# MLP up product of a GLA/gMLP block: pairs of column blocks as seven products of quarters, sums on GpSimd

## The chip, the cores and the metric

The kernel runs on one NeuronCore of a Trainium2 chip. The metric is device time of one launch in microseconds (us), the median of several runs. Engines are called as the profile calls them: PE is TensorE, DVE VectorE, ACT ScalarE, POOL GpSimd, SP SyncE, which issues most DMAs.

## The reference, cut to what matters

One layer of an encoder in float32, 256 rows (SEQ) of width 2048 (D_MODEL). The change lies in the MLP at its end:

```python
h = h + mixed @ w_out[l]
hn = rmsnorm(h, norm_mlp_w[l])
h = h + jnp.square(jax.nn.relu(hn @ w_ff_up[l])) @ w_ff_down[l]   # 2048 x 8192, 8192 x 2048
return rmsnorm(h, norm_final_w)
```

Ahead of it stand the projections of the normed input (`w_in`), a gated linear attention, a spatial gating unit, their gated merge (`w_branch`) and `w_out`.

## The kernel before

Every large product keeps float32 accuracy with three products of rounded operands: an operand is split into a high part (rounded to the `F32R` type) and a low part (the rest), and PE computes high x high, low x high and high x low into one PSUM bank. `gemm` (L188) makes one block of 512 output columns (CB) for 256 rows: 16 tiles of the inner dimension (KT), taken in pairs, and two halves of the rows (NTT), so 16 x 2 x 3 = 96 matmuls of 512 columns. The activations are the stationary operand, the weights stream.

For each pair of tiles `split_weights` (L173) loads 128 x 1024 weights by SP into a tile `w` (5 buffers), ACT casts them into `wh` (4 buffers, L182) and DVE subtracts to make `wl` (4 buffers, L183). `wh` and `wl` come free when PE has used them, so the three engines run a few pairs ahead of PE and no more.

The MLP has four stages of 2048 hidden columns. `up` (L737) makes a block of hidden columns: a `gemm` with the normed rows `hT` (the norm's weight is in `hT`, the row's factor `rstd2` is applied by ACT on the way out of PSUM with Relu), a square on DVE (L740), and jobs that turn the block into a stationary operand: 16 transposes of 32 x 256 on DVE (L271) and a split (L288 on ACT, L289 on DVE). Jobs wait in `pending`, and `gemm` runs one of them (`drain`) per pair of tiles. `down` (L750) multiplies the hidden columns of the stage before with a block of `w_ff_down` and adds the result into `h` on DVE (L755). Blocks of `up` and `down` alternate. After the first block of the kernel, a scheduler orders the instructions of each engine, and engines run their queues in order.

POOL has only small work: the powers of -0.5 in the norms (`rsqrt_of`, L309), on tiles of one or two columns, and memsets. In the spatial gating unit (L675 to L698) DVE has statistics (L685), scalings (L689), products with a weight (L694) and a split (L697) between the low parts L183.

Of the kernel before, what the change touches and what calls it, by code (L numbers as in the profile page):

```python
# [14 lines left out]
P = 128  # L15
# [24 lines left out]
W_ROW = 1088  # L40
# [18 lines left out]
def block_kernel(  # L59
# [25 lines left out]
    slots = ctx.enter_context(tc.tile_pool(name="slots", bufs=29))  # L85
# [87 lines left out]
    def split_weights(src, by_k=False):  # L173
# [6 lines left out]
        for s in [slice(i, i + 1) for i in range(k)] if by_k else [slice(0, k)]:  # L180
            nc.sync.dma_start(wv[:, s], src[:, s])  # L181
            pin(nc.scalar.copy(hv[:, s], wv[:, s]))  # L182
            pin(nc.vector.tensor_tensor(  # L183
                lv[:, s], wv[:, s], hv[:, s].bitcast(F32), op=ALU.subtract
            ))
        return hv, lv

    def gemm(a, w, c0, n=CB, parts=1, k0=0, after=None, split_tail=False):  # L188
# [5 lines left out]
        def products(kt, tt, hi, lo):  # L194
            ah, al = a.at(kt, tt)
            for i in range(parts):
                o = ps[i][tt][:, 0:m]
                wh = hi[:, kt % 2, cols(i, m)]
                wl = lo[:, kt % 2, cols(i, m)]
                pin(nc.tensor.matmul(o, lhsT=ah, rhs=wh, start=kt == 0, stop=False))  # L200
                pin(nc.tensor.matmul(o, lhsT=al, rhs=wh, start=False, stop=False))  # L201
                pin(nc.tensor.matmul(o, lhsT=ah, rhs=wl, start=False, stop=kt == KT - 1))  # L202

        for kb in range(KT // 2):
            r0 = k0 + kb * 2 * P
            hi, lo = split_weights(
                w[r0 : r0 + 2 * P, c0 : c0 + n].rearrange("(k p) n -> p k n", p=P),
                by_k=after is not None and kb == 0,
            )
# [6 lines left out]
            if split_tail and kb >= KT // 2 - 3:  # L216
# [12 lines left out]
    def to_operand_pair(dst, src, scale=None):  # L229
# [11 lines left out]
        hi, lo = dst.hi[-1], dst.lo[-1]  # L241
        if scale is None:
# [30 lines left out]
    def to_operand_vector(dst, src, scale=None):  # L273

        tr = []

        def step(jm):
            if jm == 0:
                tr.append(slot())
            transpose_quadrants(tr[0], src, jm)  # L280

        def split():
# [92 lines left out]
    vec_m = cpool.tile([NVEC, P], F32, name="vec_m")  # L375
# [418 lines left out]
    for st in range(n_st + 1):  # L794
# [48 lines left out]
```

## Time and profile before

| what | value |
|---|---|
| median of 3 runs | 1625.09 us (1625.01 to 1626.37) |
| profiled execution, its own time | 1625.84 us |
| its span, first to last instruction | 1624.1 us |
| PE busy | 1606.1 us, 99% |
| DVE busy | 1128.0 us, 69% |
| ACT busy | 755.9 us, 47% |
| POOL busy | 23.3 us, 1% |
| mean granted TensorE clock | 0.998 |

The span is what the profile's instructions cover; the time of the execution has 1.7 us around it. Busy time of PE is modelled, so the pace of PE is better read from how far apart other engines' regular work starts.

### The profile page before, as it was taken

Reading aid. Unit: us, or ns where it says so; the run is one execution under the profiler, and the core shown is the slowest. Engines: PE = TensorE matmul, PEld = TensorE weight load, DVE = VectorE, ACT = ScalarE, POOL = GpSimd, SP = SyncE. Lnnn points to the kernel's source line nnn. Section 1 sums busy time; section 2 is a strip of 40 time slices with the busy share of each in tenths; the row PEclk is TensorE's granted clock in tenths of the full one; section 3 lists DMA queues with packets and bytes.
Section 4 is the critical chain, followed back from the end, with each engine's and each line's share of the span. In section 5 each row is a group of like instructions: output and inputs, shape, how many; then the busy total and the mean of one; then the engine's idle time right before and its main releaser. Section 6 shows DMA issues by size and latency. Waiting matters only on the chain.

```text
span 1624.1 us, 19352 instructions
## 1 busy us (share of the span) xinstructions
PE 1606.1 (99%) x7224; PEld 1330.5 (82%) x7224; DVE 1128.0 (69%) x1486; ACT 755.9 (47%) x864; POOL 23.3 (1%) x50
## 2 busy tenths in 40 slices
PE   8999999999999999999999999999999999999997
PEld 6877888888888888888888888888888888888886
DVE  5759576855555788877759788876666666677754
ACT  6475444544444444544435544444444444444443
POOL 0000000000000000000000000000000000000000
PEclk9999999999999999999999999999999999999999
DMA  7655566566666666566655656655555666666653
GB/s 246 205 167 172 154 193 182 182 216 199 200 209 184 193 190 185 182 211 200 200 193 180 199 179 195 207 194 192 184 184 194 195 205 199 197 193 193 219 193 116
DMA packets 163095, 311.75 MB, mean 192 GB/s; under 512 B 9812, under 2 KB 13192, under 8 KB 163000
## 3 DMA queue, kind: packets, MB, share of 16 engines
q1 hardware_dynamic: 160016, 306.35, 60.2%
q10 hardware_dynamic: 2984, 4.16, 0.7%
q8 instruction: 56, 0.92, 0.2%
q14 instruction: 39, 0.32, 0.1%
HBM read 308.37 MB, written 2.10 MB: 191 GB/s over the span
## 4 chain that ended last, share of the span: by engine, by line
PE 97%; DVE 1%; DMA 0%; issue 0%; ACT 0%; SPq 0%; POOL 0%; ACTq 0%; POOLq 0%; DVEq 0%
PE mm L200 32%; PE mm L202 32%; PE mm L201 32%; DVE slot L271 1%; PE tr L564 1%; DVE wl L183 1%; PE tr L612 1%; DMA h<-in_x_dram 0%; PE tr L707 0%; PE tr L239 0%; ACT wh L182 0%; PE tr L467 0%; POOL col L309 0%; SPq L181 0%; PE tr L415 0%
## 5 line engine op out<-in xcount | busy, mean ns | idle before, releaser
L183 DVE TENSOR_TENSOR wl<-w,wh 128x1024 fp32r<-128x1024 f32 (+2 forms) x577 | 700.6, 1222 | 432.0 <-ACT wh L182 427.2
L182 ACT CAST wh<-w 128x1024 fp32r<-128x1024 f32 (+2 forms) x577 | 605.4, 1051 | 732.5 <-PE mm L201 683.4
L200 PE MATMUL mm<-wh,slot 128*128 128x512 f32 (+1 forms) x2336 | 905.3, 388 | 0.0
L202 PE MATMUL mm<-wl,slot 128*128 128x512 f32 (+1 forms) x2336 | 902.9, 387 | 2.3 <-DVE wl L183 2.3
L201 PE MATMUL mm<-wh,slot 128*128 128x512 f32 (+1 forms) x2336 | 902.6, 386 | 0.0
L202 PEld LDWEIGHTS mm<-wl,slot 128*128 128x128 f32 x2336 | 438.5, 188 | 93.6 <-DVE wl L183 4.5
L200 PEld LDWEIGHTS mm<-wh,slot 128*128 128x128 f32 x2336 | 438.9, 188 | 88.3 <-ACT pair L329 0.2
L201 PEld LDWEIGHTS mm<-wh,slot 128*128 128x128 f32 x2336 | 438.9, 188 | 87.8
L271 DVE STREAM_TRANSPOSE slot<-pair 32x256 f32<-32x256 f32 x496 | 216.2, 436 | 8.3
L329 ACT ACTIVATE pair<-mm,rstd 128x512 f32<-128x512 f32 x58 | 39.9, 689 | 31.6 <-PE mm L202 31.4
L288 ACT CAST slot<-slot 128x1024 fp32r<-128x1024 f32 x23 | 24.3, 1056 | 32.3 <-DVE slot L271 32.3
L309 POOL TENSOR_TENSOR col<-col,mhalf 128x1 f32<-128x1 f32 (+1 forms) x20 | 17.9, 897 | 859.8 <-DVE col L307 572.4
L289 DVE TENSOR_TENSOR slot<-slot,slot 128x1024 fp32r<-128x1024 f32 x23 | 28.0, 1219 | 0.0
L755 DVE TENSOR_TENSOR h<-mm,h 128x512 f32<-128x512 f32 x32 | 22.0, 692 | 5.3 <-PE mm L202 5.3
L271 DVE STREAM_TRANSPOSE slot<-h 32x256 f32<-32x256 f32 x48 | 21.0, 436 | 0.9
L293 ACT ACTIVATE slot<-slot,vec 128x256 fp32r<-128x256 f32 x28 | 12.1, 498 | 16.4 <-DVE slot L271 16.4
L740 DVE TENSOR_TENSOR pair<-pair 128x1024 f32<-128x1024 f32 x16 | 19.5, 1219 | 0.0
L315 ACT ACTIVATE ev<-h 128x512 f32<-128x512 f32 x24 | 15.0, 627 | 7.9 <-DVE h L755 7.9
L254 DVE SCALAR_TENSOR_TENSOR slot<-tr,mixw,slot 128x256 fp32r<-128x256 f32 x16 | 7.0, 479 | 11.2 <-ACT slot L249 11.2
L294 DVE SCALAR_TENSOR_TENSOR slot<-slot,vec,slot 128x256 fp32r<-128x256 f32 x28 | 11.8, 479 | 0.0
L249 ACT ACTIVATE slot<-tr,mixw 128x256 fp32r<-128x256 f32 x16 | 6.7, 471 | 10.6 <-PE tr L239 10.6
L710 DVE SCALAR_TENSOR_TENSOR pair<-tr,vec,pair 128x256 f32<-128x256 f32 x16 | 7.0, 479 | 6.5 <-PE tr L707 6.4
(103 smaller groups left out, 265.2 us busy)
## 6 DMA issues: line engine op xcount, KB each, us to landing
w<-in_w_in_dram SPq DMA_DIRECT2D x215, 512.0 KB, 3.7
w<-in_w_ff_up_dram SPq DMA_DIRECT2D x128, 512.0 KB, 3.7
w<-in_w_ff_down_dram SPq DMA_DIRECT2D x128, 512.0 KB, 3.5
w<-in_w_branch_dram SPq DMA_DIRECT2D x64, 512.0 KB, 3.5
w<-in_w_out_dram SPq DMA_DIRECT2D x32, 512.0 KB, 3.6
w<-in_w_in_dram SPq DMA_DIRECT2D x8, 528.0 KB, 4.6
h<-in_x_dram SPq DMA_DIRECT2D x8, 256.0 KB, 7.8
bg<-in_b_gate_dram ACTq DMA_DIRECT2D x8, 256.0 KB, 4.0
```

Source lines behind the costliest of these rows:

```text
L182: pin(nc.scalar.copy(hv[:, s], wv[:, s]))
L183: pin(nc.vector.tensor_tensor(lv[:, s], wv[:, s], hv[:, s].bitcast(F32), op=ALU.subtract))
L200: pin(nc.tensor.matmul(o, lhsT=ah, rhs=wh, start=kt == 0, stop=False))
L201: pin(nc.tensor.matmul(o, lhsT=al, rhs=wh, start=False, stop=False))
L202: pin(nc.tensor.matmul(o, lhsT=ah, rhs=wl, start=False, stop=kt == KT - 1))
L271: nc.vector.transpose(dv[cols(jm, 32), i], sv[cols(i, 32), jm])
L288: nc.scalar.copy(hi, tr[0])
L289: nc.vector.tensor_tensor(lo, tr[0], hi.bitcast(F32), op=ALU.subtract)
L309: nc.gpsimd.tensor_tensor(r, m, mhalf[:, 0:width], op=ALU.pow)
L329: nc.scalar.activation(res[:, tt, :], ps[tt], func, scale=scale[tt])
L740: nc.vector.tensor_tensor(a, a, a, op=ALU.mult)
L755: nc.vector.tensor_tensor(part, ps[tt], part, op=ALU.add)
```

## The change

The hidden columns come in eight stages of 1024 instead of four of 2048. `hidden(0)` makes the first two blocks of `up` as before. The other seven stages are made by `strassen`: the normed rows are a 2 x 2 matrix of quarters (128 rows x 1024 inner), the weights another (1024 inner x 512 columns), and their product is formed from seven products of quarters instead of eight, by Winograd's form of Strassen's scheme. Each product has 8 inner tiles and three matmuls per tile, as before, into one bank of PSUM; seven of the eight banks are in use.

The seven sums of the left side are prepared once, in jobs during the first two blocks: `norm_step` applies norm weight and row factor to kept raw rows (`raw`), `split_left` splits quarters and sums, `left_sum` makes four sums on POOL. The sums of weights are made anew in each of the four steps of a stage: POOL adds b00+b01 into `s1`, then b01+b11, b00+b01, b10+b00 in place, 128 x 1024 each; ACT casts and DVE subtracts for each of the seven products. At the end of a stage seven adds on DVE (L882) put the products together, and Relu and square are on ACT.

`down` takes 8 inner tiles at a time, so a block has 48 matmuls and there are twice as many blocks. Of its four low parts per block the last three are made on POOL (except in the last stage). In the first two blocks of `up` every second low part is on POOL. A block of 528 columns elsewhere is loaded in two halves, since the weight tile is now 1024 wide.

```diff
 C_G = 10256
 
 
-W_ROW = 1088
+W_ROW = 1024
...
+    def subtract(dst, a, b, gpsimd=False):
+        return (nc.gpsimd if gpsimd else nc.vector).tensor_tensor(dst, a, b, op=ALU.subtract)
+    def split_weights(src, by_k=False, gpsimd=False):
...
-                lv[:, s], wv[:, s], hv[:, s].bitcast(F32), op=ALU.subtract
-            ))
+            pin(subtract(lv[:, s], wv[:, s], hv[:, s].bitcast(F32), gpsimd))
         return hv, lv
...
-    def gemm(a, w, c0, n=CB, parts=1, k0=0, after=None, split_tail=False):
+    def gemm(a, w, c0, n=CB, parts=1, k0=0, nk=KT, after=None, split_tail=False, on_gpsimd=(), jobs=1):
 
...
+            src = w[r0 : r0 + 2 * P, c0 : c0 + n].rearrange("(k p) n -> p k n", p=P)
+            hi, lo = [], []
+            step = 2 if n <= CB else 1
+            for k in range(0, 2, step):
+                hv, lv = split_weights(
+                    src[:, k : k + step], by_k=after is not None and kb == 0,
+                    gpsimd=kb in on_gpsimd,
+                )
+                hi += [hv[:, i, :] for i in range(step)]
+                lo += [lv[:, i, :] for i in range(step)]
...
             if kb > 1 or kb == 1 and len(pending) > 6:
-                drain()
+                drain(jobs)
...
         hi, lo = dst.hi[-1], dst.lo[-1]
+        if keep is not None:
+            if k == 0:
+                keep.append(slot())
+            nc.scalar.copy(keep[-1][:, k : k + 2, :], tv)
...
-    def up(st, j, f):
-        ps = gemm(hT, w_ff_up[0], st * D + j * CB)[0]
-        a = scaled(ps, rstd2, AF.Relu)
-        nc.vector.tensor_tensor(a, a, a, op=ALU.mult)
-        to_operand_vector(f, a)
...
+    row_scale = ev_tile()[:, 0:T]
+    def row_scale_step():
+        tp = tr_ps()
+        for tt in range(NTT):
+            wide = ev_tile()[:, 0:P]
+            nc.scalar.activation(wide, ident, AF.Identity, scale=0.0, bias=rstd2[tt])
+            nc.tensor.matmul(tp[:, cols(tt, P)], lhsT=wide, rhs=ident, start=True, stop=True)
+        nc.vector.tensor_copy(row_scale, tp[:, 0:T])
+    def norm_step(b):
+        for k in range(4):
+            v = raw[b][:, k, :]
+            nc.vector.scalar_tensor_tensor(
+                out=v, in0=v, scalar=vcol(V_MLP + 4 * b + k), in1=row_scale,
+                op0=ALU.mult, op1=ALU.mult,
+            )
...
+    left = {}
+    def split_left(name, src):
+        hi, lo = slot(F32R), slot(F32R)
+        for s, hv, lv in zip(src, halves(hi), halves(lo)):
+            nc.scalar.copy(hv, s)
+            nc.vector.tensor_tensor(lv, s, hv.bitcast(F32), op=ALU.subtract)
+        left[name] = [t.rearrange("p a (s t) -> p (a s) t", t=P) for t in (hi, lo)]
+    sums = []
+    def left_sum(name, a, b, op):
+        if not sums:
+            sums.append(slot())
+        for d, x, y in zip(halves(sums[0]), a(), b()):
+            nc.gpsimd.tensor_tensor(d, x, y, op=op)
+        split_left(name, halves(sums[0]))
+    def last_sum():
+        return halves(sums[0])
+    prepare = [row_scale_step] + [lambda b=b: norm_step(b) for b in range(4)]
+    for i, j in ((0, 0), (0, 1), (1, 1)):
+        prepare.append(lambda i=i, j=j: split_left(f"A{i}{j}", quarter(i, j)))
+    for name, a, b, op in (
+        ("A10-A11", lambda: quarter(1, 0), lambda: quarter(1, 1), ALU.subtract),
+        ("A10-A11-A00", last_sum, lambda: quarter(0, 0), ALU.subtract),
+        ("A10-A11-A00+A01", last_sum, lambda: quarter(0, 1), ALU.add),
+        ("A00-A10", lambda: quarter(0, 0), lambda: quarter(1, 0), ALU.subtract),
+    ):
+        prepare.append(lambda name=name, a=a, b=b, op=op: left_sum(name, a, b, op))
...
+    def strassen(w, c0):
+        bank = {n: mm_ps() for n in "1235"}
+        bank.update({n: tr_ps() for n in "764"})
+        def product(i, name, a, src):
+            hi, lo = pair_of("wh", F32R, 4), pair_of("wl", F32R, 4)
+            nc.scalar.copy(hi, src)
+            subtract(lo, src, hi.bitcast(F32))
+            ah, al = left[a]
+            for kk in range(2):
+                kt = 2 * i + kk
+                for n, (x, y) in enumerate(((ah, hi), (al, hi), (ah, lo))):
+                    nc.tensor.matmul(
+                        bank[name], lhsT=x[:, kt, :], rhs=y[:, kk, :],
+                        start=kt == 0 and n == 0, stop=kt == SK - 1 and n == 2,
+                    )
+        def add(dst, x, y):
+            nc.gpsimd.tensor_tensor(dst, x, y, op=ALU.add)
+        for i in range(SK // 2):
+            b = []
+            for kh, nh in ((0, 0), (1, 0), (1, 1), (0, 1)):
+                t = ring_tile("b", 4) if kh == 0 else pair_of("w", F32, 5)
+                r0, n0 = kh * SK * P + i * 2 * P, c0 + nh * CB
+                load(t, w[r0 : r0 + 2 * P, n0 : n0 + CB].rearrange("(k p) n -> p k n", p=P))
+                b.append(t)
+            b00, b10, b11, b01 = b
+            s1 = ring_tile("s", 1)
+            add(s1, b00, b01)
+            add(b01, b01, b11)
+            product(i, "1", "A00", b00)
+            product(i, "2", "A01", b10)
+            product(i, "3", "A10-A11-A00+A01", b11)
+            product(i, "5", "A10-A11", s1)
+            add(b00, b00, b01)
+            product(i, "7", "A00-A10", b01)
+            product(i, "6", "A10-A11-A00", b00)
+            add(b10, b10, b00)
+            product(i, "4", "A11", b10)
+            drain(3)
+        p1, u2, u3, t = (ev_tile() for _ in range(4))
+        c = [pair_tile() for _ in range(2)]
+        nc.scalar.copy(p1, bank["1"])
+        for dst, x, y, op in (
+            (c[0][:, 0, :], bank["2"], p1, ALU.add),
+            (u2, bank["6"], p1, ALU.add),
+            (u3, bank["7"], u2, ALU.add),
+            (t, bank["3"], u2, ALU.subtract),
+            (c[0][:, 1, :], bank["4"], u3, ALU.add),
+            (c[1][:, 1, :], bank["5"], u3, ALU.subtract),
+            (c[1][:, 0, :], bank["5"], t, ALU.add),
+        ):
+            nc.vector.tensor_tensor(dst, x, y, op=op)
+        return c
+    def hidden(st):
+        f = Operand()
+        c0 = st * 2 * CB
+        if st == 0:
+            pending.extend(prepare)
+            for j in range(2):
+                ps = gemm(hT, w_ff_up[0], c0 + j * CB, on_gpsimd=(1, 3, 5, 7), jobs=2)[0]
+                a = scaled(ps, rstd2, AF.Relu)
+                nc.vector.tensor_tensor(a, a, a, op=ALU.mult)
+                to_operand_vector(f, a)
+        else:
+            for a in strassen(w_ff_up[0], c0):
+                nc.scalar.activation(a, a, AF.Relu)
+                nc.scalar.activation(a, a, AF.Square)
+                to_operand_vector(f, a)
+        return f
...
     def down(st, j, f):
         last = st == n_st - 1
-        ps = gemm(f, w_ff_down[0], j * CB, k0=st * D, split_tail=last and j == 3)[0]
+        ps = gemm(
+            f, w_ff_down[0], j * CB, k0=st * SK * P, nk=SK, split_tail=last and j == 3,
+            on_gpsimd=() if last else (1, 2, 3),
+        )[0]
...
+    prev = hidden(0)
+    for st in range(1, n_st + 1):
+        f = hidden(st) if st < n_st else None
...
         for j in range(4):
-            if st < n_st:
-                up(st, j, f)
-            if prev is not None:
-                down(st - 1, j, prev)
+            down(st - 1, j, prev)
```

POOL in the MLP. In the kernel before, its rows from the norm after `w_out` to the end are these (`col` is one value per row, `mhalf` the constant -0.5):

```order
L309 TENSOR_TENSOR col_7320<-col_7318,mhalf 128x1
L309 TENSOR_TENSOR col_7328<-col_7326,mhalf 128x1
L779 TENSOR_TENSOR col_12490<-col_12488,mhalf 128x1
L779 TENSOR_TENSOR col_12509<-col_12507,mhalf 128x1
```

In the changed kernel POOL's rows at the end of the first `down` stage and the start of the second Strassen stage are these (L178 is a low part, L847 a sum of weights; `slot_7808` and `slot_7904` hold b00, `slot_7814` and `slot_7910` b01, `slot_7816` is `s1`, the `w` tiles b10 and b11):

```order
L178 TENSOR_TENSOR wl_8456<-w_8454,wh_8455 128x1024
L178 TENSOR_TENSOR wl_8474<-w_8472,wh_8473 128x1024
L847 TENSOR_TENSOR slot_7816<-slot_7808,slot_7814 128x1024
L847 TENSOR_TENSOR slot_7814<-slot_7814,w_8528 128x1024
L178 TENSOR_TENSOR wl_8496<-w_8494,wh_8495 128x1024
L847 TENSOR_TENSOR slot_7808<-slot_7808,slot_7814 128x1024
L847 TENSOR_TENSOR w_8526<-w_8526,slot_7808 128x1024
L847 TENSOR_TENSOR slot_7816<-slot_7904,slot_7910 128x1024
```

The first two sums of a stage stand ahead of the last low part of `down`; from there on POOL has only sums, four a step, 16 a stage.

DVE in the MLP. In the kernel before, its rows in a block of `up` (with the jobs of the block before it) are of this kind:

```order
L183 TENSOR_TENSOR wl_8569<-w_8567,wh_8568 128x1024
L740 TENSOR_TENSOR pair_8502<-pair_8502 128x1024
L271 STREAM_TRANSPOSE slot_8550<-pair_8502 32x8x32 x8
L183 TENSOR_TENSOR wl_8591<-w_8589,wh_8590 128x1024
L271 STREAM_TRANSPOSE slot_8550<-pair_8502 32x8x32 x4
L183 TENSOR_TENSOR wl_8613<-w_8611,wh_8612 128x1024
L271 STREAM_TRANSPOSE slot_8550<-pair_8502 32x8x32 x4
```

In the changed kernel they are these at the start of the second Strassen stage (the low parts of products 1, 2, 3, 5, 7, 6, 4 in that order, then those of the next step):

```order
L178 TENSOR_TENSOR wl_8534<-slot_7808,wh_8533 128x1024
L178 TENSOR_TENSOR wl_8544<-w_8526,wh_8543 128x1024
L178 TENSOR_TENSOR wl_8554<-w_8528,wh_8553 128x1024
L918 TENSOR_TENSOR h<-mm_8434,h 128x512
L918 TENSOR_TENSOR h<-mm_8435,h 128x512
L178 TENSOR_TENSOR wl_8564<-slot_7816,wh_8563 128x1024
L178 TENSOR_TENSOR wl_8575<-slot_7814,wh_8574 128x1024
L178 TENSOR_TENSOR wl_8585<-slot_7808,wh_8584 128x1024
L178 TENSOR_TENSOR wl_8596<-w_8526,wh_8595 128x1024
L178 TENSOR_TENSOR wl_8614<-slot_7904,wh_8613 128x1024
```

Three low parts stand ahead of the last adds of `down` into `h`; after them DVE has nothing but low parts until the end of the stage, and those of products 6 (`slot_7808`) and 4 (`w_8526`) read what POOL writes. The transposes now lie between the rows of `down`.

## Rows read from the trace of the kernel before

**Rows 1.** The page: busy time by engine, and the chain that ended last.

```profile
PE 1606.1 (99%) x7224; PEld 1330.5 (82%) x7224; DVE 1128.0 (69%) x1486; ACT 755.9 (47%) x864; POOL 23.3 (1%) x50
PE 97%; DVE 1%; DMA 0%; issue 0%; ACT 0%; SPq 0%; POOL 0%; ACTq 0%; POOLq 0%; DVEq 0%
```

**Rows 2.** Timeline of DVE in the MLP: start, duration, instruction, [idle before, releaser].

```profile
1042.15 1.22 DVE L183 TENSOR_TENSOR wl<-w,wh 128x1024 fp32r<-128x1024 f32 x1
1043.29 1.22 DVE L289 TENSOR_TENSOR slot<-slot,slot 128x1024 fp32r<-128x1024 f32 x1
1044.42 2.35 DVE L183 TENSOR_TENSOR wl<-w,wh 128x1024 fp32r<-128x1024 f32 x2
...
1053.21 1.22 DVE L183 TENSOR_TENSOR wl<-w,wh 128x1024 fp32r<-128x1024 f32 x1 [1.49 <-ACT wh L182]
1055.93 1.23 DVE L183 TENSOR_TENSOR wl<-w,wh 128x1024 fp32r<-128x1024 f32 x1 [1.50 <-ACT wh L182]
1058.65 1.23 DVE L183 TENSOR_TENSOR wl<-w,wh 128x1024 fp32r<-128x1024 f32 x1 [1.49 <-ACT wh L182]
```

**Rows 3.** Windows: busy us of each engine in a stretch, granted clock, DMA.

```profile
1130.00:1216.00 86.00, 86.00 (x381) 71.22 (x380) 58.80 (x72) 36.93 (x38) 0.00 (x0) 1.00 0.61 195
```

**Rows 4.** Groups by line and shape: count, busy us, mean ns, idle before.

```profile
L182 ACT CAST wh<-w 128x1024 fp32r<-128x1024 f32 x249 | 262.3, 1053 | 334.4 <-PE mm L201 313.8 <-ACT wh L182 13.9 <-issue 2.7
L271 DVE STREAM_TRANSPOSE slot<-pair 32x256 f32<-32x256 f32 x256 | 111.7, 436 | 4.4
L755 DVE TENSOR_TENSOR h<-mm,h 128x512 f32<-128x512 f32 x30 | 20.6, 692 | 0.0
L759 DVE TENSOR_TENSOR h<-h,slot 128x512 f32<-128x512 f32 x6 | 3.9, 684 | 0.0
L294 DVE SCALAR_TENSOR_TENSOR slot<-slot,vec,slot 128x256 fp32r<-128x256 f32 x28 | 11.8, 479 | 0.0
```

**Rows 5.** The same view, of POOL.

```profile
L159 POOL MEMSET starts<- 128x1024 bf16 x1 | 1.0, 952 | 0.0
masks.py:199 POOL TENSOR_SCALAR_AFFINE_SELECT ident<-ident 128x128 f32<-128x128 f32 x1 | 0.3, 295 | 0.0
L825 POOL MEMSET const-float32-1.0<- 128x1 f32 x1 | 0.1, 103 | 0.0
```

**Rows 6.** Timeline of POOL in the spatial gating unit (third and fourth couples alike).

```profile
522.13 0.70 POOL L309 TENSOR_TENSOR col<-col,mhalf 128x2 f32<-128x2 f32 x1 [210.36 <-DVE col L307]
526.62 2.14 POOL L309 TENSOR_TENSOR col<-col,mhalf 128x2 f32<-128x2 f32 x1 [3.79 <-DVE col L307]
567.06 0.69 POOL L309 TENSOR_TENSOR col<-col,mhalf 128x2 f32<-128x2 f32 x1 [38.30 <-DVE col L307]
571.54 2.13 POOL L309 TENSOR_TENSOR col<-col,mhalf 128x2 f32<-128x2 f32 x1 [3.79 <-DVE col L307]
```

**Rows 7.** Timeline of DVE around the first couple of rows 6.

```profile
521.89 0.42 DVE L685 BATCH_NORM_STATS2 col<-pair 128x6 f32<-128x256 f32 x1
522.87 0.74 DVE L689 TENSOR_SCALAR pair<-pair,col,col 128x256 f32<-128x256 f32 x2 [0.55 <-POOL col L309]
...
526.38 1.22 DVE L183 TENSOR_TENSOR wl<-w,wh 128x1024 fp32r<-128x1024 f32 x1
527.52 0.69 DVE L697 TENSOR_TENSOR ev<-pair,ev 128x512 fp32r<-128x512 f32 x1
528.80 0.74 DVE L689 TENSOR_SCALAR pair<-pair,col,col 128x256 f32<-128x256 f32 x2 [0.59 <-POOL col L309]
```

**Rows 8.** Windows at the end of the kernel, columns as in rows 3.

```profile
1612.00:1616.00 4.00, 3.35 (x15) 2.44 (x13) 1.98 (x4) 2.06 (x4) 0.55 (x1) 1.00 0.24 90
1616.00:1620.00 4.00, 0.00 (x0) 0.00 (x0) 1.44 (x4) 2.06 (x4) 0.55 (x1) 0.86 0.76 245
1620.00:1624.00 4.00, 0.00 (x0) 0.00 (x0) 0.00 (x0) 0.00 (x0) 0.00 (x0) 0.50 0.60 189
```

**Rows 9.** The chain that ended last, at the start of the kernel: start, us, what.

```profile
9.42 0.43 PE mm L200
9.85 0.43 PE mm L201
...
11.43 0.23 PE mm L202
```

More of the change, by code (lines that the diff above doesn't have):

```diff
@@ L197, in products @@
                 o = ps[i][tt][:, 0:m]
-                wh = hi[:, kt % 2, cols(i, m)]
-                wl = lo[:, kt % 2, cols(i, m)]
+                wh = hi[kt % 2][:, cols(i, m)]
+                wl = lo[kt % 2][:, cols(i, m)]
                 pin(nc.tensor.matmul(o, lhsT=ah, rhs=wh, start=kt == 0, stop=False))
                 pin(nc.tensor.matmul(o, lhsT=al, rhs=wh, start=False, stop=False))
-                pin(nc.tensor.matmul(o, lhsT=ah, rhs=wl, start=False, stop=kt == KT - 1))
-        for kb in range(KT // 2):
+                pin(nc.tensor.matmul(o, lhsT=ah, rhs=wl, start=False, stop=kt == nk - 1))
+        for kb in range(nk // 2):
             r0 = k0 + kb * 2 * P
[L206 to L209, printed above, removed]
+            src = w[r0 : r0 + 2 * P, c0 : c0 + n].rearrange("(k p) n -> p k n", p=P)
[8 more added lines that the diff above has]
+                lo += [lv[:, i, :] for i in range(step)]
             if after is not None:
@@ L271, in transpose_quadrants, with to_operand_vector @@
             nc.vector.transpose(dv[cols(jm, 32), i], sv[cols(i, 32), jm])
-    def to_operand_vector(dst, src, scale=None):
-        tr = []
+    def to_operand_vector(dst, src, scale=None, keep=None):
+        tr = [] if keep is None else keep
         def step(jm):
@@ L730, in block_kernel @@
             nc.vector.tensor_tensor(part[:, tt], ps[tt], part[:, tt], op=ALU.add)
-        (to_operand_vector if j < 3 else to_operand)(hT, part, lambda kt: vcol(V_MLP + kt))
+        (to_operand_vector if j < 3 else to_operand)(hT, part, lambda kt: vcol(V_MLP + kt), raw)
         for tt in range(NTT):
@@ new lines, in norm_step, with quarter, halves @@
+    def norm_step(b):
[5 more added lines that the diff above has]
+            )
+    def quarter(i, j):
+        return [raw[2 * j + b][:, :, cols(i, P)] for b in range(2)]
+    def halves(t):
+        v = t.rearrange("p a (s t) -> p (a s) t", t=P)
+        return [v[:, 4 * b : 4 * b + 4, :] for b in range(2)]
+    left = {}
@@ new lines, in block_kernel, with ring_tile, pair_of @@
+    SK = 8
+    ring, turn = {}, {}
+    def ring_tile(name, n):
+        k = turn[name] = (turn.get(name, -1) + 1) % n
+        if (name, k) not in ring:
+            ring[name, k] = slot()
+        return flat(ring[name, k]).rearrange("p (k n) -> p k n", k=2)
+    def pair_of(tag, dt, bufs):
+        t = wpool.tile([P, W_ROW], dt, tag=tag, name=uid(tag), bufs=bufs)
+        return t.rearrange("p (k n) -> p k n", k=2)
+    def strassen(w, c0):
[50 more added lines that the diff above has]
+        return c
```

36 lines of the change are left out of this document (17 added, 19 removed).

## Prediction

> **What bounds the kernel now.** I read the page's busy shares and the chain that ended last first. TensorE (PE) is busy 99% of the span and holds 97% of the chain; no other engine holds over 1% [rows 1]. So a gain must come out of TensorE's own work, and a loss comes wherever another engine becomes unable to keep up with it.
>
> The pace is read from VectorE (DVE). In the MLP it makes one low part per pair of weight tiles, which serve 12 matmuls; those low parts start 2.72 us apart and DVE idles 1.49 us before each, waiting for ScalarE, which itself waits for PE [rows 2]. So a 512-column matmul costs 2.72/12 = 0.227 us, one column block of 96 matmuls 21.8 us, and one pair of blocks of up 43.5 us. A pair of up and the matching share of down (192 matmuls each) take 87.0 us; the stretch 1130 to 1216 shows PE busy in all of its 86 us at granted clock 1.00, DVE in 58.8 and GpSimd (POOL) in none [rows 3].
>
> **What is removed.** Seven of the eight pairs of blocks of up go from 192 matmuls to 7 products x 8 tiles x 3 = 168. That is 24 x 0.227 = 5.4 us a pair, 38 us in all: the most that the change can give, if nothing else is late. Down keeps its matmuls.
>
> **What is added, and where.** A Strassen stage has four steps. In a step PE has 42 matmuls (9.5 us). DVE has seven low parts of 128x1024: each is busy 1.22 us, but back to back they start 1.13 to 1.14 us apart [rows 2], so 7 x 1.14 = 8.0 us. ScalarE has seven casts of 1.05 us [rows 4], 7.4 us. GpSimd has four adds of 128x1024. So each engine by itself could stay under 9.5 us if an add costs under 2.4 us. The question is whether DVE and GpSimd work at the same time.
>
> **The price of an add.** The trace has no wide GpSimd operation with two inputs. The nearest rows: a memset of 1024 columns, which only writes, takes 0.95 us, a one-column one 0.10, so 0.83 ns a column; a select with one input takes 0.295 us for 128 columns, so 1.52 ns a column [rows 5]. One input thus adds 0.69 ns a column. My estimate for two is 0.83 + 2 x 0.69 = 2.21 ns a column, with 0.10 fixed 2.36 us; I take 2.35. Ends: 0.95 us (as the memset) and 3.2 us (twice the select). I take the middle because reading two inputs should cost more than reading one.
> The Trainium skill, "GPSIMD Engine Reference", section on performance versus the Vector engine, gives 4497 ns for an add of 2048 columns and calls elementwise work on GpSimd about twice as slow as on VectorE; half of that is 2.25 us, an estimate by that page, and the sum below would come out about 11 us lower. No run here shows it yet.
>
> **Do they overlap?** Here the trace speaks against the change. GpSimd's only two-input work is a tiny power of 128x2. The first of each couple takes 0.69 or 0.70 us; at that time DVE runs statistics with one input. The second takes 2.13 or 2.14 us, all four times [rows 6]. At 526.62 it starts 0.24 us into a low part of DVE (two inputs in SBUF, 526.38 to 527.60), which is followed at once by another such subtraction to 528.21; the power ends at 528.76, 0.55 us after that [rows 7]. So GpSimd got nothing done while DVE ran two-input instructions, and a back-to-back pair kept it out altogether. The low parts of a Strassen step are such instructions, seven in a row (the order above).
> The Trainium skill, "SBUF — State Buffer", section on who interferes with whom, says this: DVE and GpSimd share a read port as an exclusive lock, a DVE instruction with two SBUF inputs takes it against a GpSimd instruction that reads SBUF, and whichever is second blocks until the first ends. The rows agree where GpSimd is second; no row shows DVE second. With the rule the sum is the one below, with the rows alone the one-sided rival is open too.
>
> **The sum.** Counted as mutual exclusion, a step needs 7 x 1.14 + 4 x 2.35 = 17.4 us where PE needs 9.5. Followed by hand in the order of the queues, little of that is idle: while ScalarE casts one sum (1.05 us), the other engine has something. b00+b01 is made early, then b01+b11; the next two adds overwrite b00 and b10 and so wait for the low parts of products 1 and 2, and DVE's low parts of products 6 and 4 are queued behind those adds, with the next step's behind them. PE waits for the last low part.
> - Strassen stage: 4 x 17.4 = 69.5 us.
> - Of it, two adds and three low parts stand in the queues ahead of the end of down, 2 x 2.35 + 3 x 1.14 = 8.1 us. Down has room for them: its two-input work is 12 low parts on GpSimd (28.2 us), 4 on DVE and 2 splits of the operand (6.8), 35.0 of 43.5 us. DVE's 32 transposes (0.436 us) have one input and lie beside it.
> - After the last low part, PE's six matmuls, 1.4 us, before down goes on.
> - Down itself 43.5 us: hidden under it are the low parts on GpSimd, since 3 x 2.35 = 7.1 us per block is under PE's 10.9; if an add cost over 3.6 us, that cover would be gone.
> Together 69.5 - 8.1 + 1.4 + 43.5 = 106.3 us against 87.0: 19.3 us later, seven times: 135 us.
> - The first two blocks of up (not Strassen) carry the preparation. DVE: 8 low parts (9.1), 16 scalings of 128x256 at 0.40 us (0.479 busy, 0.08 less back to back; 6.4), 14 halves of splits at 0.60 (0.684 busy for such a size, likewise; 8.4), 2 squares (2.3), 26.2 us. GpSimd: 8 low parts (18.8) and 8 half sums of 512 columns, 0.10 + 512 x 2.21 ns = 1.23 us (9.8), 28.6 us. 54.8 us against PE's 43.5: 11 us later [rows 4]. The first Strassen stage therefore has nothing pre-run (8 us) and two splits more (2 us).
> - At nothing: 8 loads cut in two, the 22 us of additional adds into h (32 x 0.69, one of their inputs in PSUM), the casts that keep the raw rows; they lie on DVE and ScalarE under PE's work, where both idle at that time. Weight traffic per us falls with the longer stage, so DMA does not bind.
> Sum on the profiled execution: 1625.8 + 135 + 11 + 8 + 2 = 1782 us (its span is 1624.1, with 1.7 outside; the median of the runs is 0.7 lower). With the add at 3.2 us, down's own 45.2 us go over PE's and nothing is pre-run: a cycle of 129.7 us, 1950 in all. At 0.95 us a cycle is 86.7, some 1630 in all.
>
> **Rivals.**
> *One-sided exclusion.* An add waits until DVE's run of low parts ends, but DVE doesn't wait for an add that has begun. Then a step is the adds (9.4 us) and between half and all of one run of four low parts (2.3 to 4.6): 11.7 to 14 us. A cycle is 84 to 93 us, the whole 1615 to 1675; middle 1650. For it: only GpSimd's waiting is in the rows. Against it: two operands have to come from somewhere while the other engine reads.
> *The clock falls too.* PE would be busy only 55% of a Strassen stage. In the rows the granted clock is 1.00 wherever PE works, also with short waits; it is 0.86 and 0.50 only in the last 8 us, in which PE does nothing [rows 8]. At the lower level a matmul takes 0.43 us, as the first ones of the kernel do [rows 9]; then PE alone needs 18.1 us a step, a step with the waits about 19, a cycle 115, the whole about 1845. Against it: the waits in a step should be 1 to 3 us pieces, not 8.
> *The other side: the adds hide.* If a wide add streams beside DVE's low parts, or costs under about 0.97 us (there 69.5 shrinks until the cycle is 87.0), PE stays the bound: 38.1 + 1.4 + 43.5 = 83.0 us a cycle, 4 us less, 7 times, 1598 us. For it: the power is a slow operation on a tiny tile and may suffer more than a stream. Against it: its body ran whole after DVE's, four times of four.
>
> **Chances and range.** Mutual exclusion at full clock 0.60 (its own range 1700 to 1850, by an add of 1.8 to 2.8 us), with the lower clock 0.17, one-sided 0.13, hidden adds 0.10. The prediction is that of the first, 1782 us. The range 1640 to 1870 leaves out the hidden adds, the lower half of the one-sided case and the far end of the add's price. Slower by over 0.2% (3.3 us, about what a measurement here can tell from no change): the first two and most of the third, 0.87; the hidden adds and the lowest one-sided cases are faster, 0.11; in between 0.02.
>
> **What the profile after would show.** Right: GpSimd and DVE busy in turn through a Strassen stage, their times together filling it; a step of about 17 us; PE busy some 55% there, waiting for low parts and sums; GpSimd's low parts in down well over 2.4 us when DVE is at two-input work; down's stretches still full on PE. Wrong: low parts and adds at their lone durations side by side, or PE still 99% busy; an add under 1 us; a granted clock near 0.5 in those stages; or down's stretches getting longer, which would mean that low parts on GpSimd come late for PE there too.

## The result and the profile after

The changed kernel takes 1832.38 us (median of 4 runs, 1831.56 to 1837.21) where the kernel before, on the same chip, takes 1625.61 (4 runs): a ratio of 1.1277 [1.1263, 1.1291], 206.8 us slower. The forecast was 1782 us, in a range of 1640 to 1870, by mutual exclusion of VectorE and GpSimd.

The page of the changed kernel, with the lines that answer to [rows 1] and the rows of PE, POOL and the granted clock in 40 slices of the span:

```profile
span 1830.3 us, 19759 instructions
PE 1629.9 (89%) x7060; PEld 1309.5 (72%) x7060; DVE 1415.3 (77%) x1584; ACT 863.5 (47%) x981; POOL 633.9 (35%) x262
PE   8999999999999999999986697786968869787698
...
POOL 0000000000000000000066667677776777767750
PEclk9999999999999999999998898999999999998999
...
PE 73%; DVE 15%; issue 7%; POOL 4%; DMA 1%; ACT 1%; DVEq 0%; SPq 0%; POOLq 0%; ACTq 0%
```

PE is no longer on the whole chain: its row drops below 9 just where POOL's row begins, in the MLP. DVE and POOL have taken 19% of the chain, and 7% more is put down to issue (time in which an engine waited for nothing that the profile shows).

One Strassen stage and the share of `down` that follows it are called a cycle here. The pace of the MLP is read from the adds that close each Strassen stage (the view of line 882: count, shortest, median and longest ns, first and last start, shape). There is one such row per stage, so six cycles lie between the first and the last:

```profile
L882 DVE TENSOR_TENSOR ev<-mm,ev x7: 679/681/681, 1062.3 to 1735.6; 128x512 f32<-128x512 f32 x7
```

(1735.6 - 1062.3) / 6 = 112.2 us a cycle, against the 87.0 worked out from [rows 2, 3]. Cut at that row and at the second power of `rstd2`, the spans of the two profiles differ like this (of the kernel before, a cycle's worth of the same blocks stands at 87.0 us, and the rest is what remains):

| piece | before | after | difference | forecast |
|---|---|---|---|---|
| start to the power of `rstd2` | 921.5 | 925.3 | +3.8 | 0 |
| to the end of the first Strassen stage | 87.0 | 137.0 | +50.0 | +40 |
| six cycles | 6 x 87.0 | 6 x 112.2 | +151 | +116 |
| the rest | 93.6 | 94.7 | +1.1 | 0 |

Within a Strassen step the forecast can be checked instruction by instruction. The timelines of POOL and of DVE in a middle stage (start, duration, instruction, idle before):

```profile
1125.74 3.25 POOL L847 TENSOR_TENSOR slot<-slot,slot 128x1024 f32<-128x1024 f32 x1 [3.50 <-DVE wl L178]
1129.08 3.24 POOL L847 TENSOR_TENSOR w<-w,slot 128x1024 f32<-128x1024 f32 x1
1133.48 3.32 POOL L847 TENSOR_TENSOR slot<-slot,slot 128x1024 f32<-128x1024 f32 x1 [1.16 <-DVE wl L178]
1136.88 3.25 POOL L847 TENSOR_TENSOR slot<-slot,w 128x1024 f32<-128x1024 f32 x1
1142.49 3.25 POOL L847 TENSOR_TENSOR slot<-slot,slot 128x1024 f32<-128x1024 f32 x1 [2.37 <-DVE wl L178]
```

```profile
1133.32 4.56 DVE L178 TENSOR_TENSOR wl<-slot,wh 128x1024 fp32r<-128x1024 f32 x2
1137.80 3.41 DVE L178 TENSOR_TENSOR wl<-w,wh 128x1024 fp32r<-128x1024 f32 x1
1141.13 1.21 DVE L178 TENSOR_TENSOR wl<-slot,wh 128x1024 fp32r<-128x1024 f32 x1
1142.27 1.21 DVE L178 TENSOR_TENSOR wl<-w,wh 128x1024 fp32r<-128x1024 f32 x1
```

The sum into b00 (the first of POOL's rows) comes again 1142.49 - 1125.74 = 16.75 us later; a step was forecast at 17.4. The fourth of POOL's rows runs from 1136.88 to 1140.13. DVE's low part is issued into it at 1137.80 and ends at 1141.21, 1.08 us after the add: its own 1.14 us of work begins when the add is over. So DVE is held as second engine too, which the rows before could not show ([rows 6, 7] had only GpSimd as second). The low parts behind it, with no add beside them, take 1.21 us as in [rows 2].

The windows (busy us of PE, PEld, DVE, ACT and POOL with counts, granted clock, DMA share, GB/s) of two steps, of a stretch of `down`, and of the end of that `down`:

```profile
1125.70:1142.50 16.80, 11.03 (x45) 7.84 (x44) 16.80 (x8) 7.53 (x8) 13.07 (x5) 1.00 0.51 178
1142.50:1159.20 16.70, 10.64 (x43) 7.53 (x42) 16.70 (x8) 7.30 (x8) 13.06 (x4) 1.00 0.34 124
1170.40:1212.50 42.10, 40.63 (x178) 33.03 (x177) 35.22 (x52) 21.10 (x22) 29.70 (x12) 1.00 0.67 212
1214.00:1222.00 8.00, 2.19 (x9) 1.56 (x8) 5.03 (x2) 1.05 (x1) 7.92 (x4) 0.77 0.33 127
1222.00:1230.00 8.00, 8.00 (x30) 6.37 (x29) 4.55 (x4) 3.42 (x4) 6.13 (x3) 0.80 0.01 2
```

In a step DVE counts as busy for all of it and POOL for 13 us, but these are times from issue to end, the other's lock included: by the lone durations only 7 x 1.14 + 4 x 2.38 = 17.5 us of work is there, for both together. PE works 11 of 16.8 us, at granted clock 1.00. Down is still PE's (40.6 of 42.1 us), until its end.

### The profile page after: what moved, and what is told of

It reads as the page before. It is cut to its first block, busy times and chain, and to the rows that moved or that the text cites. A ratio compares the mean times of both kernels' runs of the same rounds, so it can differ in the third digit from the quotient of the medians.

```text
span 1830.3 us, 19759 instructions
## 1 busy us (share of the span) xinstructions
PE 1629.9 (89%) x7060; PEld 1309.5 (72%) x7060; DVE 1415.3 (77%) x1584; ACT 863.5 (47%) x981; POOL 633.9 (35%) x262
## 4 chain that ended last, share of the span: by engine, by line
PE 73%; DVE 15%; issue 7%; POOL 4%; DMA 1%; ACT 1%; DVEq 0%; SPq 0%; POOLq 0%; ACTq 0%
PE mm L207 21%; PE mm L205 21%; PE mm L206 20%; DVE wl L178 13%; PE mm L841 6%; POOL wl L178 3%; PE tr L841 3%; DVE slot L286 1%; PE tr L579 1%; PE tr L627 0%; POOL slot L847 0%; DMA w<-in_w_in_dram 0%; PE tr L722 0%; PE tr L250 0%; ACT wh L189 0%
## 5 line engine op out<-in xcount | busy, mean ns | idle before, releaser
L178 DVE TENSOR_TENSOR wl<-w,wh 128x1024 fp32r<-128x1024 f32 (+2 forms) x465 | 698.9, 1513 | 266.2 <-ACT wh L189 252.7
L207 PE MATMUL mm<-wl,slot 128*128 128x512 f32 (+1 forms) x1888 | 740.3, 392 | 62.9 <-POOL wl L178 45.6
L205 PE MATMUL mm<-wh,slot 128*128 128x512 f32 (+1 forms) x1888 | 738.1, 391 | 2.6 <-ACT pair L459 2.5
L206 PE MATMUL mm<-wh,slot 128*128 128x512 f32 (+1 forms) x1888 | 734.9, 389 | 0.0
L189 ACT CAST wh<-w 128x1024 fp32r<-128x1024 f32 (+2 forms) x473 | 485.9, 1035 | 464.7 <-PE mm L206 408.0
L178 POOL TENSOR_TENSOR wl<-w,wh 128x1024 fp32r<-128x1024 f32 x92 | 256.7, 2812 | 368.4 <-ACT wh L189 368.4
L178 DVE TENSOR_TENSOR wl<-slot,wh 128x1024 fp32r<-128x1024 f32 x112 | 232.9, 2110 | 21.7 <-ACT wh L835 21.3
L847 POOL TENSOR_TENSOR slot<-slot,slot 128x1024 f32<-128x1024 f32 x56 | 166.2, 2967 | 119.8 <-DVE wl L178 103.3
L835 ACT CAST wh<-slot 128x1024 fp32r<-128x1024 f32 x112 | 117.7, 1051 | 161.5 <-PE mm L206 70.1
L841 PE MATMUL mm<-wl,slot 128*128 128x512 f32 x224 | 95.3, 426 | 62.2 <-DVE wl L178 62.2
L841 PE MATMUL mm<-wh,slot 128*128 128x512 f32 x448 | 144.4, 405 | 1.7 <-ACT wh L835 1.7
L841 PE MATMUL tr<-wl,slot 128*128 128x512 f32 x168 | 70.7, 421 | 54.3 <-DVE wl L178 54.3
L841 PEld LDWEIGHTS mm<-wl,slot 128*128 128x128 f32 x224 | 43.6, 195 | 90.6 <-DVE wl L178 82.4
L841 PE MATMUL tr<-wh,slot 128*128 128x512 f32 x336 | 105.6, 394 | 1.2 <-ACT wh L835 1.2
L841 PEld LDWEIGHTS mm<-wh,slot 128*128 128x128 f32 x448 | 88.5, 198 | 20.1 <-ACT wh L835 2.1
L847 POOL TENSOR_TENSOR slot<-slot,w 128x1024 f32<-128x1024 f32 x28 | 89.9, 3209 | 2.2
```

What stands on the lines that cost most here:

```text
L178: return (nc.gpsimd if gpsimd else nc.vector).tensor_tensor(dst, a, b, op=ALU.subtract)
L835: nc.scalar.copy(hi, src)
L841: nc.tensor.matmul(bank[name], lhsT=x[:, kt, :], rhs=y[:, kk, :], start=kt == 0 and n == 0, stop=kt == SK - 1 and n == 2,)
L847: nc.gpsimd.tensor_tensor(dst, x, y, op=ALU.add)
```

## The experiments

The first four ran on one chip beside the kernel before (1625.37 us there).

**1. The sums on DVE.** Same work, no GpSimd in the Strassen stages.

```diff
         def add(dst, x, y):
-            nc.gpsimd.tensor_tensor(dst, x, y, op=ALU.add)
+            nc.vector.tensor_tensor(dst, x, y, op=ALU.add)
```

> The four sums of weights of each Strassen step are on VectorE instead of GpSimd; nothing else changes. Theory (two-input work of GpSimd and VectorE excludes itself, so a step is the sum of both): a step is 11 x 1.14 = 12.5 us instead of the 16.75 us of the changed kernel, a cycle of one Strassen stage and one share of down about 94 us instead of 112.8, the whole about 1700 us, although all the work now lies on the engine that was already the busier one. Rival (the engines work side by side, and VectorE is simply the bound in these stages): more work on VectorE makes it slower, 1850 us or more. Every other part stays, the low parts of down on GpSimd too.

Measured: 1720.68 us, ratio 1.0582 [1.0564, 1.0599]. That is some 20 us over what was expected. Giving DVE four more instructions a step, and taking them from an otherwise idle engine, saves 112 us. Had GpSimd run beside DVE, this could have helped only by shortening a chain of waits through the slower engine, the rival that run 4 takes up; by exclusion the two are one resource, on which an add costs 2.4 us by GpSimd and 1.14 by DVE. The cycle is 95.8 us.

**2. Nothing of the MLP on GpSimd.** As 1, and the low parts of `down` and of the first blocks and the sums of the left side on DVE too.

```diff
-            on_gpsimd=() if last else (1, 2, 3),
...
-                ps = gemm(hT, w_ff_up[0], c0 + j * CB, on_gpsimd=(1, 3, 5, 7), jobs=2)[0]
+                ps = gemm(hT, w_ff_up[0], c0 + j * CB, jobs=2)[0]
...
-            nc.gpsimd.tensor_tensor(d, x, y, op=op)
+            nc.vector.tensor_tensor(d, x, y, op=op)
```

> Nothing wide is on GpSimd: sums of weights, sums of the left side, and all low parts of up and down are on VectorE. Theory (exclusion): again a step of 12.5 us; the low parts of down cost VectorE 12 x 1.14 = 13.7 us more per share of down, which then has about 45 us of VectorE for 43.5 us of TensorE, but the wait of TensorE for a late low part of GpSimd at the end of down (6.6 us) goes. A cycle of 93 to 97 us, the whole 1680 to 1710. Rival (GpSimd relieves VectorE, as its adds and low parts lie beside VectorE's work): clearly slower than the first experiment and than the changed kernel, 1850 us or more.

Measured: 1708.55 us, ratio 1.051 [1.0494, 1.0525]: inside, near the upper end. The window of one cycle says what binds now:

```profile
1135.00:1230.00 95.00, 87.36 (x364) 66.35 (x362) 94.29 (x110) 51.14 (x53) 0.00 (x0) 1.00 0.53 178
```

DVE is busy 94.29 of 95.00 us, so the scheme is bound by VectorE once GpSimd is out.

**3. No sums of weights.**

```diff
-            s1 = ring_tile("s", 1)
-            add(s1, b00, b01)
-            add(b01, b01, b11)
...
-            product(i, "5", "A10-A11", s1)
-            add(b00, b00, b01)
+            product(i, "5", "A10-A11", b01)
...
-            add(b10, b10, b00)
```

> The four sums of weights of each step are left out; the seven products take plain quarters, so the result is not the reference's. Low parts, casts, matmuls, loads and the low parts of down on GpSimd stay. Theory: a step is bound by TensorE (9.5 us against 8.0 of VectorE), a cycle 83 to 86 us; the preparation during the first two blocks still costs 10 to 20 us; the whole 1610 to 1640. Rival (the stages lose their time to the scheme itself: seven banks, the putting together of the products, the change between stages): still over 1700.

Measured: 1624.26 us, ratio 0.9992 [0.9982, 1.0001]. The adds on GpSimd, with all that waits for them, thus cost 1832.4 - 1624.3 = 208 us, all of the loss; the cycle is 82.65 us, where the rival of hidden adds had 83.0.

**4. Low parts with one operand in PSUM.** The adds stay on GpSimd; only where DVE reads its second operand changes, and an instruction becomes two of half the width.

```diff
+        zero = tr_ps()
+        nc.vector.memset(zero, 0.0)
...
-            subtract(lo, src, hi.bitcast(F32))
+            for k in range(2):
+                subtract(lo[:, k, :], src[:, k, :], zero)
```

> The sums stay on GpSimd. The low part of each product is made in two halves as quarter minus a bank of PSUM that holds zeros, so VectorE reads one input from SBUF and one from PSUM; it takes VectorE 2 x 0.6 us instead of 1.14. The result is not the reference's (the low part is the whole quarter), and the low part no longer waits for the cast. Theory (exclusion by the second SBUF input): adds and low parts lie side by side, adds take their lone 2.36 us, a step falls from 16.75 us to 10 to 12, the whole to 1640 to 1700. Rival (the chain of four dependent adds, or waits between engines, sets the step whatever VectorE reads): no change, about 1830.

Measured: 1667.98 us, ratio 1.0266 [1.0248, 1.0284]. DVE does a little more here than in the changed kernel (14 x 0.60 = 8.4 us a step by starts, not 7 x 1.14 = 8.0), and 164 us are gone. GpSimd's adds in the changed kernel and in this one (groups by shape: count, busy us, mean ns, idle before):

```profile
L847 POOL TENSOR_TENSOR slot<-slot,slot 128x1024 f32<-128x1024 f32 x56 | 166.2, 2967 | 119.8 <-DVE wl L178 103.3 <-DMA slot<-in_w_ff_up_dram 16.5
```

```profile
L178 DVE TENSOR_TENSOR wl<-slot,tr 128x512 fp32r<-128x512 f32 x224 | 142.0, 682 | 17.6 <-PE mm L207 12.2
...
L850 POOL TENSOR_TENSOR slot<-slot,slot 128x1024 f32<-128x1024 f32 x56 | 134.7, 2405 | 47.3 <-DVE wl L178 25.7 <-DMA slot<-in_w_ff_up_dram 18.6 <-ACT wh L837 1.5
```

An add and the DVE instructions beside it, in the timelines:

```profile
1090.76 2.42 POOL L850 TENSOR_TENSOR slot<-slot,slot 128x1024 f32<-128x1024 f32 x1 [1.39 <-DVE wl L178]
```

```profile
1089.35 3.66 DVE L178 TENSOR_TENSOR wl<-slot,tr 128x512 fp32r<-128x512 f32 x6
```

The adds take 2405 ns, their lone duration, beside DVE instructions with two inputs: what excludes them is two inputs in SBUF. This is the most direct run, since the adds, their engine and their place stay; half the width and the missing wait for the cast can move the start of a low part, but neither explains that an add beside it takes no longer than alone. The cycle is 88.3 us. In six cycles PE waits 28.3 us for low parts on POOL in `down`, 1.5 us for one on DVE, and not once in a step: without the exclusion the steps are PE's again, and 4.7 of the 5.6 us by which the cycle is longer than run 3's are these waits in `down`, treated below.

**5. The last low part of each `down` on DVE**, since it is queued on POOL behind two pre-run sums. This and the next three ran on a second chip (kernel before 1625.91 us).

```diff
-            on_gpsimd=() if last else (1, 2, 3),
+            on_gpsimd=() if last else (1, 2, 3) if j < 3 else (1, 2),
```

> The changed kernel, but in the fourth block of each share of down the last low part is on VectorE instead of GpSimd, where it stood behind two sums of the next stage. Theory: the wait of TensorE for it (5.4 us each, seven times) and the half clock after it (about 2 us each) go, and GpSimd's 2.4 us become 1.14 us; the sums still have to share with VectorE, so not all of that is gained: a cycle of 105 to 108 us instead of 112.2, the whole 1785 to 1805 us. Rival (the stages are so full of two-input work that a wait only moves to another place): 1820 us or more.

Measured: 1813.47 us, ratio 1.1154 [1.1139, 1.1169], between the two. What PE waited for, over six cycles of the changed kernel (total us, times, longest):

```profile
PE mm L841 <- DVE wl L178: 50.8, 36, 1.7
PE tr L841 <- DVE wl L178: 45.2, 30, 1.7
PE mm L207 <- POOL wl L178: 38.1, 7, 6.6
PE mm L207 <- DVE wl L178: 8.8, 6, 1.5
```

and over six cycles of this one:

```profile
PE tr L841 <- DVE wl L178: 67.6, 42, 1.7
PE mm L841 <- DVE wl L178: 54.5, 42, 1.7
PE mm L207 <- DVE wl L178: 8.8, 6, 1.5
PE mm L207 <- POOL wl L178: 0.7, 1, 0.7
```

The wait for GpSimd's low part is gone (38.1 to 0.7 us), but the waits inside the steps (L841) grow from 96.0 to 122.1 us: two sums of a stage that were made while DVE stood idle behind that wait (from 1221.40) now lie against its low parts. Those of products 5, 7, 6 and 4 then take 12.2 us from the first start to the last end, and took 9.3 in the changed kernel. Net 11.3 us; another 6 x 1.9 = 11 us is the clock after the wait (below; the granted clock is 1.00 at that place here). Together 22.7 us for 6 x (112.2 - 108.5) = 22 us.

**6. GpSimd out of the first two blocks only.** Two of the edits of 2:

```diff
-                ps = gemm(hT, w_ff_up[0], c0 + j * CB, on_gpsimd=(1, 3, 5, 7), jobs=2)[0]
+                ps = gemm(hT, w_ff_up[0], c0 + j * CB, jobs=2)[0]
...
-            nc.gpsimd.tensor_tensor(d, x, y, op=op)
+            nc.vector.tensor_tensor(d, x, y, op=op)
```

> The changed kernel, but in the first two blocks of up all low parts, and the four sums of the left side, are on VectorE; from the first Strassen stage on nothing is changed. Theory (GpSimd starves behind VectorE's long run of two-input preparation, one of its low parts takes 9.58 us there, and costs the common port twice what VectorE needs): about 12 us less, 1812 to 1826 us. Rival (the preparation is simply too much for VectorE, and GpSimd relieves it): the same or slower, 1832 us or more.

Measured: 1822.54 us, ratio 1.1207 [1.119, 1.1224]: as expected. The piece up to the end of the first Strassen stage shrinks from 137.0 to 128.8 us.

**7. The scheme alone.** The edits of 3 and of 2 together: no sums of weights, and nothing of the MLP on GpSimd; of these,

```diff
-            add(b01, b01, b11)
...
-            on_gpsimd=() if last else (1, 2, 3),
```

> No sums of weights (the products take plain quarters, so the result is not the reference's) and nothing wide on GpSimd at all; low parts, left sums, casts, matmuls and loads stay. It asks what the scheme could give if the sums cost nothing and nothing shared a port. Theory: a cycle stays near TensorE's 82.7 us, the first blocks lose 10 to 14 us less than in the third experiment (1624 us), the whole 1608 to 1618 us. Rival (in down VectorE needs GpSimd's help, its 44 us of work there being over TensorE's 43.5): no gain or slower, 1624 to 1645 us.

Measured: 1619.82 us, ratio 0.9965 [0.9952, 0.9979]; a little above what was expected. Its cycle is 82.9 us, 4.1 below the kernel before, 25 us in six cycles. Most of it goes back in the preparation (first Strassen stage ended 99.8 us after the power, 13 us later than the work of before; DVE busy 90.56 of 100 us there) and in the halves:

```profile
925.00:1025.00 100.00, 89.86 (x360) 69.81 (x359) 90.56 (x126) 59.79 (x73) 0.45 (x1) 0.93 0.48 155
```

**8. The kernel before with the 528-column block in halves.**

```diff
-W_ROW = 1088
+W_ROW = 1024
...
+            step = 2 if n <= CB else 1
+            for k in range(0, 2, step):
```

> The kernel before, with one small part of the change alone: weight tiles 1024 wide, so the one block of 528 columns is loaded, cast and subtracted in two halves per pair of tiles. The prediction put this at nothing. Theory from the trace after (TensorE waits 2.5 us at the end of that block and then runs at the lower clock for a while): 3 to 5 us slower, 1628 to 1630 us. Rival (that wait comes from another order of the queues, not from the halves): no difference, 1625 us.

Measured: 1629.84 us, ratio 1.0022 [1.0012, 1.0031]: 4 us (2 to 5 by the interval) for the 8 loads cut in two.

**9. DVE relieved of the transposes.** As 2, and the hidden columns are transposed on PE, as elsewhere in the kernel. It ran on a third chip (kernel before 1625.09 us).

```diff
-                to_operand_vector(f, a)
+                to_operand(f, a)
```

> The second experiment (nothing wide on GpSimd), and the blocks of up are turned into operands by TensorE's transposes into PSUM, as the last block of the product before is, instead of by VectorE's 32 x 256 transposes. Theory (with GpSimd out of it VectorE alone bounds a cycle of 94.7 us, being busy in 94.3 of 95): VectorE loses 2 x (7.0 + 1.2) us and gains 4 x 0.68 us a cycle, so some 80.6 us are left, TensorE gains 16 transposes of 0.11 us, 82.9 + 1.8 = 84.7 us, and becomes the bound again; a cycle of 85 to 87 us, the first blocks some 8 us less, the whole 1630 to 1655 us: the scheme then costs about what it saves. Rival (a chain of waits between the engines holds the cycle, not VectorE's load; or the one bank of PSUM left for transposes holds it): 1670 us or more.

Measured: 1677.99 us, ratio 1.0322 [1.0305, 1.034]. A miss: I expected 1630 to 1655, since DVE's mean over a cycle falls well below PE's. The time lies where the rival had it, over 1670, and the cycle is 91.4 us. The window of a cycle and two pieces of DVE's timeline, one in `down` and one in a Strassen step:

```profile
1130.00:1220.00 90.00, 85.23 (x365) 65.49 (x364) 77.62 (x78) 48.39 (x50) 0.00 (x0) 1.00 0.56 183
```

```profile
1153.84 1.23 DVE L178 TENSOR_TENSOR wl<-w,wh 128x1024 fp32r<-128x1024 f32 x1 [1.49 <-ACT wh L189]
...
1188.39 1.22 DVE L847 TENSOR_TENSOR slot<-slot,slot 128x1024 f32<-128x1024 f32 x1
1189.52 1.22 DVE L178 TENSOR_TENSOR wl<-w,wh 128x1024 fp32r<-128x1024 f32 x1
1190.66 1.22 DVE L847 TENSOR_TENSOR slot<-slot,w 128x1024 f32<-128x1024 f32 x1
```

DVE is busy only 77.62 of 90 us, yet in the Strassen stage it runs back to back (11 x 1.14 = 12.5 us a step, PE needs 9.5) and in `down` it idles 1.49 us before a low part, as in [rows 2]. There it waits for ScalarE's cast, and ScalarE waits for PE to free one of the four `wh` buffers; they let it run ahead by a few pairs, so a stage's bound is not averaged with the next stage's. The rival's two reasons don't show: in the stage DVE has no idle time to fill, and PE's waits, 5.0 us over 1130 to 1225, are for casts and low parts, none for a transpose's bank.

## Why the prediction was right, and where it was 50 us short

**The mechanism stood.** "Do they overlap?" was decided from two powers of 128x2 ([rows 6, 7]) and held for wide instructions: runs 1 and 4 avoid the exclusion in the steps in two different ways and recover 112 and 164 us; run 3 shows that the adds are the whole loss. The Trainium skill, "SBUF — State Buffer", section on who interferes with whom, has the lock for whichever engine is second; the 3.41 us low part agrees with it, and run 4 with its condition of two SBUF inputs.

**The price of an add** was forecast at 2.35 us from a memset and a select [rows 5]; an add with nothing in SBUF against it took 2.40 us (run 4). The Trainium skill, "GPSIMD Engine Reference", section on performance versus the Vector engine, gave 2.25 us, an estimate by halving its figure: 0.15 us too low here.

**The step** was 16.75 us, not 17.4; by 7 x 1.14 + 4 x 2.38 = 17.5, 0.75 us less than full exclusion. I take this to be the fixed parts of the eleven instructions, 0.07 us each, lying beside the other engine's body; no run separates them.

**The rivals.** One-sided exclusion falls with the 3.41 us low part and the 16.75 us step (it had 11.7 to 14). Hidden adds fall with run 1. That the clock falls too is mostly wrong: in the middle steps it is 1.00, with 66 waits of at most 1.7 us over six cycles. Its 1845 us is nearer to the measured 1832 than the forecast, by luck: its step was 19 us. But the clock did fall after a longer wait, next, and around the first Strassen stage.

**The credit of 8.1 us failed.** The step said that two adds and three low parts are made ahead under `down`, which "has room for them", with only 1.4 us behind the last low part. Four steps and a `down`, 4 x 16.75 + 43.5 = 110.5 us, are already 1.7 below the 112.2 measured: nothing of the credit is left. POOL and PE at the end of a `down`, in the timelines:

```profile
1212.48 2.39 POOL L847 TENSOR_TENSOR slot<-slot,slot 128x1024 f32<-128x1024 f32 x1 [2.32 <-DMA slot<-in_w_ff_up_dram]
1214.95 3.20 POOL L847 TENSOR_TENSOR slot<-slot,w 128x1024 f32<-128x1024 f32 x1
1218.12 3.32 POOL L178 TENSOR_TENSOR wl<-w,wh 128x1024 fp32r<-128x1024 f32 x1
```

```profile
1215.29 0.39 PE L206 MATMUL mm<-wh,slot 128*128 128x512 f32 x1
1221.49 0.79 PE L207 MATMUL mm<-wl,slot 128*128 128x512 f32 x1 [5.81 <-POOL wl L178]
...
1222.93 0.63 PE L207 MATMUL mm<-wl,slot 128*128 128x512 f32 x1
1223.36 0.63 PE L205 MATMUL mm<-wh,slot 128*128 128x512 f32 x1
```

The sums did run ahead, and the last low part of `down` stood behind them. PE waited 5.81 us for it, and then started matmuls 0.43 us apart, as at the lower of the two levels (1.2 of 2.4 GHz; granted 0.80 over the window from 1222), for some 4 us: 1.9 us more. ([rows 9] have the same 0.43 us, but the clock granted from 8 to 12 us is 1.00, so they gave the pace and not the level.) What was gained ahead was paid in the wait. The order shown ahead of the prediction had this low part behind two adds; I counted POOL's room over the whole of `down`, not at its end, where the queue decides. That is 5.9 us a cycle, 35 of the 50 us. It would be 8.5 us, had each step not been forecast 0.65 us too long: so far the nearness of the sum is luck. The prediction's last sign of being wrong, low parts on GpSimd that come late for PE in `down`, did show here. Run 5 moved the low part, and half of its gain went into the steps instead, so neither of the two orders gets the credit in full.

**The first two blocks** and the Strassen stage behind them were 10 us dearer than forecast (+50 for +40). A low part on POOL beside the preparation on DVE:

```profile
937.18 9.58 POOL L178 TENSOR_TENSOR wl<-w,wh 128x1024 fp32r<-128x1024 f32 x1 [4.74 <-ACT wh L189]
```

```profile
930.07 8.59 DVE L767 SCALAR_TENSOR_TENSOR slot<-slot,vec,ev 128x256 f32<-128x256 f32 x16
938.58 2.49 DVE L785 TENSOR_TENSOR slot<-slot,slot 128x512 fp32r<-128x512 f32 x4
940.99 1.22 DVE L178 TENSOR_TENSOR wl<-w,wh 128x1024 fp32r<-128x1024 f32 x1
942.12 1.28 DVE L785 TENSOR_TENSOR slot<-slot,slot 128x512 fp32r<-128x512 f32 x2
943.33 1.21 DVE L178 TENSOR_TENSOR wl<-w,wh 128x1024 fp32r<-128x1024 f32 x1
```

DVE's train of two-input instructions ends at 944.54, POOL's low part at 946.76, 2.22 us later: it got in nothing until the train was over. My sum added the two engines' work but had no term for who is served last. That is only a part of the 10 us: PE waited 1.50 us for this low part, and 12.4 us in all for the low parts of the two blocks, 7.5 for those on POOL and 4.9 for those on DVE. The blocks took 62.0 us to the second square (987.35) where 54.5 were forecast, the stage behind them 75.0 for 72.9. In both, PE's granted clock fell, which the sum had at full:

```profile
971.00:990.00 19.00, 12.18 (x37) 8.85 (x38) 12.52 (x18) 5.20 (x7) 7.91 (x5) 0.81 0.35 121
990.00:1058.00 68.00, 46.98 (x161) 32.61 (x162) 67.67 (x46) 29.94 (x31) 45.74 (x15) 0.90 0.27 93
```

Run 6 takes GpSimd out there and gains 10 us, but it does not tell the order of service from the price: by the sum alone DVE's work is then 40 us, under PE's 43.5, and 11 us should go. Its blocks still take 53.8 us. How the 10 us divide stays open.

**"At nothing"** was wrong for the loads cut in two: 4 us (run 8), in the piece before the MLP. The additional adds into `h` and the casts did stay hidden: run 3, which has both, keeps a cycle of 82.65 us, and ahead of the MLP the +3.8 us is no more than run 8's.

**What is removed**, 38 us at most, was right as a bound: 4.1 us a cycle in run 7, with its preparation and halves taking most of it. No version of the scheme that makes the layer's result beats the kernel before; the best is run 9, at 1.0322 (run 4, with its sums but without the true low parts, is at 1.0266). Sums with one operand in PSUM were not tried: seven of eight banks are in use.

## What to carry to other kernels

Before moving elementwise work from VectorE to GpSimd, count the two-input SBUF instructions of both as one engine's work, each at its own engine's price, and ask which of them stands last in the queue; idle time on GpSimd is no room while VectorE runs such instructions. Count per stage, over no more work than the buffers let an engine run ahead, since a mean over a cycle hides a stage that is bound elsewhere (run 9). A scheme that saves an eighth of one product's matmuls on PE has to find its sums on engines that have time in just that stage.

## What the runs showed of the hardware that was not expected

- In the first blocks a train of two-input DVE instructions, back to back, shut GpSimd out for all of its length: a low part of 2.4 us took 9.58. In the steps it was otherwise: the add issued at 1133.48 got in after one low part (3.32 us), and DVE's next low part waited for it (the two took 4.56 us, for 2.35 in [rows 2]); adds and low parts then took turns. What tells the two cases apart no run shows.
- One-input work shared freely: beside two GpSimd low parts at their lone 2.38 us, 16 of DVE's transposes took 7.18 us, 0.449 us each, where eight in the kernel before took 3.58 us, 0.448 each:

```profile
1179.98 7.18 DVE L286 STREAM_TRANSPOSE slot<-pair 32x256 f32<-32x256 f32 x16
```

```profile
1181.73 4.76 POOL L178 TENSOR_TENSOR wl<-w,wh 128x1024 fp32r<-128x1024 f32 x2 [2.86 <-ACT wh L189]
```

- TensorE kept granted clock 1.00 through the middle steps, in which it worked 11 of 16.8 us with waits of at most 1.7 us, and came back at 0.43 us a matmul after a wait of 5.81 us. In the first stage, with waits of up to 2.6 us, it was granted 0.90 (990 to 1058).
